# Mixer projections u, b and the two gates as feature-major seven-product units on 256 tokens each

## The chip, the cores and the metric

The kernel runs on one core of one Trainium2 chip. The metric is the device time of one execution in microseconds (us). A core has a matrix engine (TensorE; PE in the profile, with its weight loads counted apart as PEld), a vector engine (VectorE, DVE), a scalar engine (ScalarE, ACT), a general engine (GpSimd, POOL) and a queue engine for transfers (SyncE, SP), which run side by side and wait for each other through semaphores. Products land in PSUM, which this kernel divides into 8 tiles of 128 x 512 float32.

## The reference, cut to what matters

512 tokens of 1024 features go through two attention layers, a feed-forward block, a mixer and a second feed-forward block. The change is in the mixer alone:

```python
z = h @ w_in                      # h: 512 x 1024, w_in: 1024 x 7168
za, zb, zg = split(z)             # u, v | gate_b, gate_c, xb | g_a, g_b, each 1024 wide
u, v = split(gelu(za))
y_a = spatial_gating(u, v) @ w_proj_a
y_b = (gate_b * short_conv(gate_c * xb)) @ w_proj_b
merged = sigmoid(g_a) * y_a + sigmoid(g_b) * y_b
out = merged @ w_out
```

## The kernel before, in words

Every float32 factor is held as two parts, a rounded one (`hi`) and what is left (`lo`). `mm3` makes a product from three matmuls of the same shape: hi x hi, hi x lo, lo x hi. Weights come from HBM in pieces of 1 MB into a ring of 5 raw tiles (`raw`). ScalarE writes `hi`, VectorE writes `lo = raw - hi`, each in tiles of 128 x 1024 with 4 buffers for each kind.

Two ways of making a projection stand in the mixer:

- Direct and feature-major (`fm1`): a weight block of 128 x 128 is stationary and all 512 tokens of the activations move past it. One output tile of 128 features is 8 x 3 matmuls of 512 columns in one PSUM tile. In before, u (`u_job`), gate_b (`b_job`) and both gates (`gated_job`) are made so. `gated_job` loads the gate's block and the block of `w_proj_a` or `w_proj_b` in one piece.
- In seven products instead of eight (`block_jobs`): the activations and weights are cut two by two, sums of blocks are formed, and seven products give the four result blocks. In before, v and gate_c with xb (`v_unit`, `cx_unit`) are made so, token-major, with 512 columns moving. The sums of activation blocks (`bt`, `bn`, and one that is put over part of `xg` by `t4_parts`) are there already. Since u, b and the gates need `xg` as it was, `block_b12` writes that part back at the end of the second `cx_unit`.

`run` walks through a list of jobs. Before it issues a job's products it asks for the next job's weights. Small pieces of other work (`light`: the spatial gate, convolutions, transposes) are put in between at due times. The order of the list in the mixer is v, cx 0, cx 1, u, first gate with `w_proj_a`, b, second gate with `w_proj_b`, output. A planner then fixes each engine's order of instructions ahead of time, by a simulated timeline. It may put an instruction that is ready by that timeline ahead of one that isn't, and the order is kept on the chip. Temporary tiles of 128 x 512 come from a pool of 50 slots.

Of the kernel before, what the change touches and what calls it, by code (L numbers as in the profile page):

```python
# [41 lines left out]

NCOL = _layout()
ORDER = ('gv0 gv2 dz0 gq gz0 gz2 dz2', 'gk gv0 dz2 gv2 gq dz0 gz0 gz2')
SLOTS = 50
LAG = 1
GAP = (2.6, 2.0)
AHEAD = 10.0
# [24 lines left out]
TURN = 10.0  # L73
TURN0 = 1.5
REST = 12.0


@with_exitstack
def block_kernel(ctx: ExitStack, tc: tile.TileContext, a, out):
# [64 lines left out]
    def weights(src, shapes):  # L144

        total = sum(k * n for k, n in shapes)
        raw = wraw.tile([P, 2112], F32, tag="raw", name=nm("raw"))
        nc.sync.dma_start(raw[:, 0:total], src)
        at, pieces = 0, []
        for k, n in shapes:  # L150
            src_p = raw[:, at:at + k * n]
            hi = wsp.tile([P, 1024], F32R, tag="hi", name=nm("hi"))[:, 0:k * n]
            lo = wsp.tile([P, 1024], F32R, tag="lo", name=nm("lo"))[:, 0:k * n]
            A.activation(hi, src_p, AF.Copy)  # L154
            V.tensor_tensor(lo, src_p, f(hi), op=ALU.subtract)  # L155
            pieces.append(tuple(v.rearrange("p (k n) -> p k n", n=n) for v in (hi, lo, src_p)))
            at += k * n
        return pieces

    FM = [(KT, P)] * 2  # L160
    TM = [(2, S)] * 2
# [192 lines left out]
        A.activation(hi, e, AF.Copy)  # L354
        V.tensor_tensor(lo, e, f(hi), op=ALU.subtract)

    def block(name, p, t):

        tiles, at = {
            "b11": (lambda: st["xg"][2 * p], 0), "b21": (lambda: st["xg"][2 * p + 1], 0),  # L360
            "b22": (lambda: st["xg"][2 * p + 1], H), "t4": (lambda: st["xg"][2 * p], H),
            "t3": (lambda: st["bt"][p], 0), "t2": (lambda: st["bt"][p], H),
            "t1": (lambda: st["bn"][p // 2], p % 2 * H),
        }[name]
        return tuple(v[:, at + t * P:at + t * P + P] for v in tiles())

    def block_b12(p, nxt):

        hi, lo = (v[:, H:] for v in st["xg"][2 * p])
        x, g = xs[2 * p][:, H:], nxt(2 * p)  # L370
        A.activation(hi, x, AF.Copy, scale=g)
        V.scalar_tensor_tensor(lo, x, g, f(hi), op0=ALU.mult, op1=ALU.subtract)

    def block_jobs(src, hook, turn=False):


        q, banks = {}, {}

        def load(name, i):
            q[name] = wraw.tile([P, 2112], F32, tag="raw", name=nm("raw"))[:, 0:4 * S]  # L380
            nc.sync.dma_start(q[name], src[i])

        def parts(name, turn=False):
            pieces = []
            for j in range(2):
                r = q[name][:, 2 * j * S:2 * j * S + 2 * S]
                hi, lo = (wsp.tile([P, 1024], F32R, tag=v, name=nm(v)) for v in ("hi", "lo"))
                A.activation(hi, r, AF.Copy)  # L388
                if turn:
                    A.activation(lo, r, AF.Copy, scale=-1.0)  # L390
                    nc.gpsimd.dma_start(lo, r, accum_op=ALU.add)
                else:
                    V.tensor_tensor(lo, r, f(hi), op=ALU.subtract)  # L393
                pieces.append(tuple(v.rearrange("p (k n) -> p k n", n=S) for v in (hi, lo)))
            return pieces

        def l1():
            load("a11", 0)
            load("a21", 2)
            nc.gpsimd.dma_start(q["a21"], q["a11"], accum_op=ALU.add)  # L400
            return parts("a11", turn)

        def l2():
            load("a22", 3)
            return parts("a21")

        def l3():
            load("a12", 1)
            return parts("a21")

        def sums(i):

            if i == 0:
                V.tensor_tensor(q["a21"], q["a21"], q["a22"], op=ALU.add)
            if i == 1:
                V.tensor_tensor(q["a11"], q["a21"], q["a11"], op=ALU.subtract)

        def l4():
            nc.gpsimd.dma_start(q["a21"], q["a12"], accum_op=ALU.add)
            return parts("a11")  # L420


        steps = [
            (l1, "b11", "a", True), (l2, "t3", "b", True), (l3, "t2", "a", False), (l4, "t1", "a", False),
            (lambda: parts("a12"), "b21", "c", True), (lambda: parts("a22"), "t4", "b", False),
            (lambda: parts("a21"), "b22", "a", False),
        ]

        def step(i, name, chain, first):
            def body(ps):  # L430
                if first:
                    banks[chain] = [psum("tm") for _ in range(2)]
                for t in range(2):
                    for p in range(4):
                        ah, al = block(name, p, t)
                        wh, wl = (v[:, p % 2] for v in ps[p // 2])
                        mm3(banks[chain][t], ah, al, wh, wl, first and p == 0, p == 3, True)
                        yield 0.68
                    hook(i, t, banks)
                    if t == 0:  # L440
                        sums(i)
            return body

        return [(ld, None, step(i, *which)) for i, (ld, *which) in enumerate(steps)]


    mods = [(const.tile([P, 24], F32, name=f"mod{l}"), const.tile([P, 8], F32, name=f"gs{l}")) for l in range(L)]
# [788 lines left out]
    def mixer_jobs():  # L1236
# [66 lines left out]
        def cx_unit(n):  # L1303
            v, h = {}, {}

            def hook(i, t, banks):
# [6 lines left out]
                if i == 5:  # L1313
                    V.scalar_tensor_tensor(v[0, t], v[2, t], roots("nrs2", t), v[0, t], op0=ALU.mult, op1=ALU.mult)
                    h[t] = v[0, t]
                    if t == 1 and n == 1:
                        for p in range(4):
                            block_b12(p, gains)
                if i == 6:
                    V.scalar_tensor_tensor(v[3, t], v[3, t], roots("nrs2", 2 + t), banks["a"][t], op0=ALU.mult, op1=ALU.mult)  # L1320
                    h[2 + t] = v[3, t]
# [1 line left out]
                        light(conv(n, h), TURN)  # L1323

            return block_jobs(a["mcx"][n], hook)

        jobs += v_unit()
        for n in range(2):
            jobs += cx_unit(n)

        def gate(h, u):
            b, hb = h // 4, slice((h % 4) * P, (h % 4 + 1) * P)
# [8 lines left out]
            ya[h] = split(u, "ya")  # L1341
            yield 0.9, 0

        def u_job(c):
            def body(ps):
                if c == 0:
                    spatial()
                for j in range(2):
                    h = 2 * c + j
                    o = psum("fm")  # L1350
                    yield from fm1(o, [ps[j]], st["xg"])
                    u = slot("mu")
                    V.tensor_tensor(u, o, st["bc"], op=ALU.mult)
                    A.activation(u, u, AF.Gelu_apprx_tanh)
                    light(gate(h, u), 9.0 if h < 2 else 2.0)
            return body

        jobs += [(a["mu"][c], FM, u_job(c)) for c in range(4)]


        def gated_job(which, i, acts):
            def body(ps):
                o = psum("fm")
                yield from fm1(o, [ps[0]], st["xg"])
                t = slot("mgt")
                V.tensor_tensor(t, o, st["bc"], op=ALU.mult)
                A.activation(t, t, AF.Tanh, scale=0.5)
                while len(acts) < KT:
                    yield None
                pr = psum("fm")  # L1370
                yield from fm1(pr, [ps[1]], acts)
                V.scalar_tensor_tensor(t, t, 1.0, pr, op0=ALU.add, op1=ALU.mult)
                if which == 0:
                    ma.append(t)
                else:
                    V.tensor_tensor(t, t, ma[i], op=ALU.add)
                    mer.append(split(t, "mm"))
            return body

        jobs += [(a["mgp"][0, i], FM, gated_job(0, i, ya)) for i in range(KT)]  # L1380

        def b_job(c):
            def body(ps):
                for j in range(2):
                    o = psum("fm")
                    yield from fm1(o, [ps[j]], st["xg"])
                    g = slot("mgb")
                    V.tensor_tensor(g, o, st["bc"], op=ALU.mult)
                    while len(cv) <= 2 * c + j:
                        yield None  # L1390
                    V.tensor_tensor(g, g, cv[2 * c + j], op=ALU.mult)
                    yb.append(split(g, "yb"))
            return body

        jobs += [(a["mb"][c], FM, b_job(c)) for c in range(4)]
        jobs += [(a["mgp"][1, i], FM, gated_job(1, i, yb)) for i in range(KT)]

        def o_job(c):
            def body(ps):
# [19 lines left out]
def _pack(i):  # L1419
# [65 lines left out]
    w = i["w_in_2"][0]  # L1485
    mu, mv, mb, mc, mx, ga, gb = (w[:, D * j:D * j + D] for j in range(7))
    r["mv"] = c(blocks(mv[:, 0:S], mv[:, S:]))
    r["mu"], r["mb"], r["mo"] = c(cols256(mu)), c(cols256(mb)), c(cols256(i["w_out_2"][0]))

    def pairs(p, q):  # L1490
        return np.stack([tiles(np.concatenate([p[:, P * j:P * j + P], q[:, P * j:P * j + P]], axis=1)) for j in range(8)])

    r["mcx"] = c(np.stack([blocks(mc[:, j:j + S], mx[:, j:j + S]) for j in (0, S)]))
    r["mgp"] = c(np.stack([pairs(ga, i["w_proj_a_2"][0]), pairs(gb, i["w_proj_b_2"][0])]))
    r["sgu_wT"] = c(i["sgu_w_2"][0].transpose(2, 0, 1).reshape(P, 2, 4 * P).transpose(1, 0, 2))
    r["sgu_b"] = c(i["sgu_b_2"][0])
    return r
# [18 lines left out]
```

## Time and profile before

| | |
|---|---|
| median of 3 runs | 1693.03 us (1692.37 to 1694.29) |
| the profiled execution | 1691.1 us |
| its span, first to last instruction | 1689.3 us |
| TensorE busy | 1647.6 us, 98% of the span, 8080 matmuls |
| VectorE busy | 1127.6 us, 67% |
| ScalarE busy | 807.7 us, 48% |
[...]

Busy time is the time in which the engine had at least one instruction in work, as the profiler's records say. The records of matmuls overlap (one lasts longer than the distance to the next), so the pace of matmuls is read from their starts or from their number in a stretch, not from the duration of one. In the trace the mixer lies from about 905 us (first v product) to about 1339 us.

### The profile page before, as it was taken

How to read it: one execution, taken by the hardware profiler on the slowest of the kernel's cores; microseconds unless marked ns; L12 is line 12 of the kernel's file. 1: busy time of each engine (PE TensorE's matmuls, PEld its weight loads, DVE VectorE, ACT ScalarE, POOL GpSimd, SP SyncE). 2: the span in 40 equal slices, each digit the busy share in tenths (PEclk: the TensorE clock that was granted, in tenths of full speed). 3: DMA queues.
4: the chain of work that ended last, by engine and by line, in shares of the span. 5: the costliest groups of instructions: out<-in, count | busy, mean ns of one | idle time of the engine just before them, and what ended most of it. 6: DMA issues, size and time to landing. Idle time of an engine off the chain costs nothing.

```text
span 1689.3 us, 20507 instructions
## 1 busy us (share of the span) xinstructions
PE 1647.6 (98%) x8080; PEld 1363.9 (81%) x8080; DVE 1127.6 (67%) x1648; ACT 807.7 (48%) x1343; POOL 113.6 (7%) x102
## 2 busy tenths in 40 slices
PE   6997999999999999999999999999999999999998
PEld 5785788897778888888888888888888888888887
DVE  8889866778765865755768887534545775765754
ACT  4564565446655543533556654322233553542543
POOL 3120010330000000000002100000000000000000
PEclk9998999999999999999999999999999999999999
DMA  8535412342213163553554653222222334561521
GB/s 313 202 131 194 163 63 76 126 150 75 75 51 94 50 181 115 159 165 97 151 161 109 165 173 126 79 96 100 100 100 100 93 109 122 149 199 51 162 88 50
DMA packets 32161, 209.73 MB, mean 124 GB/s; under 512 B 3617, under 2 KB 3777, under 8 KB 8641
## 3 DMA queue, kind: packets, MB, share of 16 engines
q1 hardware_dynamic: 28032, 180.11, 29.8%
q0 software_dynamic: 4032, 28.31, 8.7%
q8 instruction: 63, 1.03, 0.2%
q14 instruction: 34, 0.27, 0.0%
HBM read 178.00 MB, written 2.10 MB: 107 GB/s over the span
## 4 chain that ended last, share of the span: by engine, by line
PE 91%; DVE 4%; ACT 2%; DMA 1%; issue 0%; POOL 0%; SPq 0%; POOLq 0%; DVEq 0%; ACTq 0%
PE fm L179 16%; PE fm L181 16%; PE fm L180 16%; PE tm L179 12%; PE tm L181 12%; PE tm L180 12%; PE ht L1100 1%; PE sc L838 1%; DVE ada L482 1%; PE o L874 1%; DVE cv L598 1%; DVE lo L155 1%; DMA ada<-in_ada 1%; PE go L994 0%; PE ot L537 0%
## 5 line engine op out<-in xcount | busy, mean ns | idle before, releaser
L154 ACT ACTIVATE hi<-raw 128x1024 fp32r<-128x1024 f32 (+2 forms) x184 | 187.9, 1024 | 350.5 <-PE fm L180 277.1
L393 DVE TENSOR_TENSOR lo<-raw,hi 128x1024 fp32r<-128x1024 f32 x180 | 218.2, 1223 | 89.4 <-ACT hi L388 88.0
L388 ACT ACTIVATE hi<-raw 128x1024 fp32r<-128x1024 f32 x182 | 191.4, 1057 | 174.4 <-PE tm L181 89.7
L155 DVE TENSOR_TENSOR lo<-raw,hi 128x1024 fp32r<-128x1024 f32 (+2 forms) x184 | 216.6, 1179 | 44.2 <-ACT hi L154 37.5
L179 PE MATMUL tm<-hi,xgh 128*128 128x512 f32 x480 | 177.9, 393 | 12.4 <-ACT hi L639 12.4
L180 PE MATMUL tm<-lo,xgh 128*128 128x512 f32 x480 | 187.7, 393 | 0.2 <-DVE lo L640 0.2
L181 PE MATMUL tm<-hi,xgl 128*128 128x512 f32 x480 | 185.2, 392 | 0.0
L179 PE MATMUL fm<-fhh,hi 128*128 128x512 f32 (+1 forms) x368 | 140.0, 383 | 0.0
L180 PE MATMUL fm<-fhl,hi 128*128 128x512 f32 (+1 forms) x368 | 139.9, 380 | 0.0
L181 PE MATMUL fm<-fhh,lo 128*128 128x512 f32 (+1 forms) x368 | 139.9, 380 | 0.0
L179 PE MATMUL fm<-xgh,hi 128*128 128x512 f32 x320 | 125.9, 393 | 0.0
L180 PE MATMUL fm<-xgl,hi 128*128 128x512 f32 x320 | 124.4, 389 | 0.0
L181 PE MATMUL fm<-xgh,lo 128*128 128x512 f32 x320 | 124.4, 390 | 0.0
L179 PEld LDWEIGHTS tm<-hi,xgh 128*128 128x128 f32 x480 | 90.4, 189 | 31.7 <-ACT hi L639 12.9
L179 PE MATMUL fm<-hh,hi 128*128 128x512 f32 x256 | 108.8, 428 | 6.8 <-DVE gs L487 4.5
L180 PEld LDWEIGHTS tm<-lo,xgh 128*128 128x128 f32 x480 | 91.1, 190 | 19.7 <-DVE lo L640 0.7
L181 PEld LDWEIGHTS tm<-hi,xgl 128*128 128x128 f32 x480 | 90.9, 190 | 18.8
L181 PE MATMUL fm<-hh,lo 128*128 128x512 f32 x256 | 103.1, 403 | 0.0
L180 PE MATMUL fm<-hl,hi 128*128 128x512 f32 x256 | 102.9, 402 | 0.0
L181 PEld LDWEIGHTS fm<-fhh,lo 128*128 128x128 f32 x368 | 69.2, 188 | 13.2
L180 PE MATMUL tm<-lo,bth 128*128 128x512 f32 x208 | 79.9, 392 | 0.0
L180 PEld LDWEIGHTS fm<-fhl,hi 128*128 128x128 f32 x368 | 69.3, 188 | 12.7
(313 smaller groups left out, 3434.0 us busy)
## 6 DMA issues: line engine op xcount, KB each, us to landing
raw<-in_ffs SPq DMA_DIRECT2D x40, 1024.0 KB, 5.0
raw<-raw POOLq DMA_DIRECT2D x26, 1024.0 KB, 8.0
ada<-in_ada SPq DMA_DIRECT2D x23, 1024.0 KB, 4.8
raw<-in_wfm SPq DMA_DIRECT2D x16, 1024.0 KB, 4.8
raw<-in_ffo SPq DMA_DIRECT2D x16, 1024.0 KB, 4.9
raw<-in_mgp SPq DMA_DIRECT2D x16, 1024.0 KB, 4.8
raw<-in_wo SPq DMA_DIRECT2D x8, 1024.0 KB, 4.8
raw<-in_mcx SPq DMA_DIRECT2D x8, 1024.0 KB, 5.8
```

The costliest lines, as they stand in the source:

```text
L154: A.activation(hi, src_p, AF.Copy)
L155: V.tensor_tensor(lo, src_p, f(hi), op=ALU.subtract)
L179: T.matmul(o, wh, ah, start=start, stop=False, skip_group_check=open)
L180: T.matmul(o, wh, al, start=False, stop=False, skip_group_check=open)
L181: T.matmul(o, wl, ah, start=False, stop=stop, skip_group_check=open)
L388: A.activation(hi, r, AF.Copy)
L393: V.tensor_tensor(lo, r, f(hi), op=ALU.subtract)
L482: V.scalar_tensor_tensor(w[:, i], w[:, i], 1.0, cact, op0=ALU.mult, op1=ALU.mult, accum_out=t[:, j + i:j + i + 1])
L598: V.scalar_tensor_tensor(c[:, sh:S], ps[:, 0:S - sh], tap[3 - sh], c[:, sh:S], op0=ALU.mult, op1=ALU.add)
L838: T.matmul(pss[m][:, 0:n], qk[hd][0][p][r, i * P:(i + 1) * P], qk[hd][1][q_][r, 0:n], start=p + q_ == 0, stop=False)
L874: T.matmul(on[hd][:, i * P:(i + 1) * P], et[:, j * P:(j + 1) * P], vt[j][:, hd * P:(hd + 1) * P], start=j == 0, stop=j == i)
L1100: T.transpose(ps[:, t * P:(t + 1) * P], h[t][:, c * P:(c + 1) * P], ident)
```

## The change

u, b and the two gates (16 pieces of 256 output features) become feature-major units of seven products, `fm_unit`. A unit holds a weight piece in four quarters: input features in even and odd blocks of 128, and two blocks of 128 output features. Each product is 4 input blocks x 3 matmuls, with a weight block of 128 x 128 stationary and 256 tokens moving (`block` gets a width). The sums of weight quarters are made by two accumulating transfers of GpSimd's queue, 256 KB each, and two subtractions and additions of VectorE. Three PSUM tiles x, y, z take the seven products in the order x, y, x, z, x, y, x, and in between x, y and z are read out and combined into two result tiles of 512 tokens.

The projections `w_proj_a` and `w_proj_b` become pieces and jobs of their own (`plain`, `p_job`), still made directly with 512 columns. The order becomes v, then u and first gate mixed (`UG`), `w_proj_a`, cx 0, cx 1, b, second gate, `w_proj_b`, output. Each item's transfer is issued inside the item before it (`linked`). `block_b12` goes. The pool grows from 50 to 56 slots, and the scratch area for GpSimd's transfer descriptors is set to 4096 bytes to make room. The amounts loaded from HBM stay the same.

The core of the diff:

```diff
-SLOTS = 50
+SLOTS = 56
+UG = ('u0', 'u1', 'g0', 'u2', 'g1', 'u3', 'g2', 'g3')
...
-        return tuple(v[:, at + t * P:at + t * P + P] for v in tiles())
-
-    def block_b12(p, nxt):
-
-        hi, lo = (v[:, H:] for v in st["xg"][2 * p])
-        x, g = xs[2 * p][:, H:], nxt(2 * p)
-        A.activation(hi, x, AF.Copy, scale=g)
-        V.scalar_tensor_tensor(lo, x, g, f(hi), op0=ALU.mult, op1=ALU.subtract)
+        return tuple(v[:, at + t * P:at + t * P + n] for v in tiles())
...
+    def fm_unit(src, begin, finish):
+        q, v = {}, {}
+
+        def parts(at, n):
+            r = q["r"][:, at:at + n]
+            hi, lo = (wsp.tile([P, 1024], F32R, tag=t, name=nm(t))[:, 0:n] for t in ("hi", "lo"))
+            A.activation(hi, r, AF.Copy)
+            V.tensor_tensor(lo, r, f(hi), op=ALU.subtract)
+            return tuple(w.rearrange("p (k n) -> p k n", n=P) for w in (hi, lo))
+
+        def quarter(i):
+            return q["r"][:, i * S:(i + 1) * S]
+
+        def load():
+            q["r"] = wraw.tile([P, 2112], F32, tag="raw", name=nm("raw"))[:, 0:4 * S]
+            nc.sync.dma_start(q["r"], src)
+            nc.gpsimd.dma_start(quarter(1), quarter(0), accum_op=ALU.add)
+
+        def first():
+            a = parts(0, 2 * S)
+            V.tensor_tensor(quarter(1), quarter(1), quarter(3), op=ALU.add)
+            V.tensor_tensor(quarter(0), quarter(1), quarter(0), op=ALU.subtract)
+            q["s"] = parts(0, 2 * S)
+            return a, q["s"]
+
+        def second():
+            a = parts(2 * S, 2 * S)
+            nc.gpsimd.dma_start(quarter(1), quarter(2), accum_op=ALU.add)
+            return a, parts(S, S)
+
+        def product(o, w, at, name, start):
+            for p in range(4):
+                ah, al = block(name, p, 0, H)
+                mm3(o, w[0][:, at + p], w[1][:, at + p], ah, al, start and p == 0, p == 3, True)
+                if p % 2:
+                    yield 0.72
+
+        def one(ps):
+            begin()
+            for k in "xyz":
+                v[k] = psum("fu")[:, 0:H]
+            v[0], v[1] = slot("fa"), slot("fb")
+            yield from product(v["x"], ps[0], 0, "b11", True)
+            A.activation(v[0][:, 0:H], v["x"], AF.Copy)
+            yield from product(v["y"], ps[0], 4, "t3", True)
+            yield from product(v["x"], ps[1], 4, "t2", False)
+            A.activation(v[1][:, 0:H], v["x"], AF.Copy, scale=-1.0)
+
+        def two(ps):
+            yield from product(v["z"], ps[0], 0, "b21", True)
+            V.tensor_tensor(v[0][:, 0:H], v[0][:, 0:H], v["z"], op=ALU.add)
+            yield from product(v["x"], q["s"], 0, "t1", False)
+            A.activation(v[1][:, H:], v["x"], AF.Copy, scale=-1.0)
+            V.tensor_tensor(v[1][:, H:], v[1][:, H:], v["y"], op=ALU.subtract)
+            yield from product(v["y"], ps[0], 4, "t4", False)
+            V.tensor_tensor(v[1][:, 0:H], v[1][:, 0:H], v["y"], op=ALU.subtract)
+            yield from product(v["x"], ps[1], 0, "b22", False)
+            yield from finish(v[0], v["x"], v[1])
+
+        return load, [(first, None, one), (second, None, two)]
...
+    def rooted(u, last, v):
+        V.tensor_tensor(u[:, 0:H], u[:, 0:H], st["bc"][:, 0:H], op=ALU.mult)
+        V.tensor_tensor(u[:, H:], last, st["bc"][:, H:], op=ALU.mult)
+        V.tensor_tensor(v, v, st["bc"], op=ALU.mult)
...
-                    if t == 1 and n == 1:
-                        for p in range(4):
-                            block_b12(p, gains)
...
+        def u_unit(c):
+            def finish(u, last, v):
+                rooted(u, last, v)
+                for j, t in enumerate((u, v)):
+                    A.activation(t, t, AF.Gelu_apprx_tanh)
+                    light(gate(2 * c + j, t), 9.0 if c == 0 else 2.0)
+                yield 0
+            return fm_unit(a["mu"][c], spatial if c == 0 else lambda: None, finish)
...
+        def g_unit(which, c):
+            def finish(u, last, v):
+                if which == 1 and c > 1:
+                    for k in range(0, 2) if c == 2 else range(2, KT):
+                        yb.append(split(cv[k], "yb"))
...
+                rooted(u, last, v)
+                for t in (u, v):
+                    A.activation(t, t, AF.Tanh, scale=0.5)
+                    gates[which].append(t)
...
+        def b_unit(c):
+            def finish(u, last, v):
+                rooted(u, last, v)
...
+                for k, t in ((2 * c, u), (2 * c + 1, v)):
+                    V.tensor_tensor(cv[k], cv[k], t, op=ALU.mult)
...
+        items = [(None, v_unit())]
+        for which in UG:
+            items.append((u_unit if which[0] == "u" else lambda c: g_unit(0, c))(int(which[1])))
+        items += [plain(a["mp"][0, c], p_job(0, c, ya)) for c in range(4)]
+        items += [(None, cx_unit(n)) for n in range(2)]
+        items += [b_unit(c) for c in range(4)] + [g_unit(1, c) for c in range(4)]
+        items += [plain(a["mp"][1, c], p_job(1, c, yb)) for c in range(4)]
+        jobs += linked(items)
...
-    nc = bacc.Bacc("TRN2", target_bir_lowering=False, num_devices=1)
+    nc = bacc.Bacc("TRN2", target_bir_lowering=False, num_devices=1, dynamic_dma_scratch_size=4096)
```

## Rows read from the trace of the kernel before

**Rows 1.** The page, part 1: busy us (share of the span), instructions.

```profile
span 1689.3 us, 20507 instructions
PE 1647.6 (98%) x8080; PEld 1363.9 (81%) x8080; DVE 1127.6 (67%) x1648; ACT 807.7 (48%) x1343; POOL 113.6 (7%) x102
```

**Rows 2.** Stretches of the mixer: length, busy us (instructions) of PE, PEld, DVE, ACT, POOL, clock.

```profile
943.00:981.00 38.00, 38.00 (x169) 31.45 (x168) 28.21 (x31) 23.14 (x29) 3.66 (x5) 1.00 0.59 167
981.00:1018.00 37.00, 37.00 (x173) 30.54 (x172) 31.39 (x36) 19.84 (x26) 0.86 (x1) 1.00 0.55 171
1077.00:1164.00 87.00, 87.00 (x385) 72.03 (x384) 31.25 (x33) 21.64 (x25) 0.00 (x0) 1.00 0.26 92
```

**Rows 3.** Waits of PE from 525 to 1665 us: the only row.

```profile
PE tm L179 <- ACT bth L169: 1.0, 1, 1.0
```

**Rows 4.** Groups of matmuls by shape: busy us, mean ns of one.

```profile
L179 PE MATMUL fm<-xgh,hi 128*128 128x512 f32 x320 | 125.9, 393 | 0.0
L180 PE MATMUL fm<-fhl,hi 128*128 128x256 f32 x32 | 9.1, 285 | 0.0
```

**Rows 5.** The stretch of the last job's 54 matmuls of 256 columns.

```profile
1665.41:1671.88 6.47, 6.47 (x55) 6.46 (x54) 2.66 (x5) 2.12 (x5) 0.00 (x0) 1.00 0.01 3
```

**Rows 6.** Timeline of PE in the first cx unit: start, us, instruction.

```profile
957.77 0.62 PE L179 MATMUL tm<-hi,xgh 128*128 128x512 f32 x2
958.22 0.39 PE L179 MATMUL tm<-hi,bnh 128*128 128x512 f32 x1
...
960.71 0.39 PE L181 MATMUL tm<-hi,bnl 128*128 128x512 f32 x1
960.94 0.39 PE L180 MATMUL tm<-lo,xgh 128*128 128x512 f32 x1
```

**Rows 7.** Groups of DVE instructions in the mixer, by shape.

```profile
L155 DVE TENSOR_TENSOR lo<-raw,hi 128x1024 fp32r<-128x1024 f32 x60 | 73.4, 1223 | 7.6 <-ACT hi L154 7.3
...
L1337 DVE SCALAR_TENSOR_TENSOR mw<-sg,cols,sgub 128x512 f32<-128x512 f32 x8 | 6.0, 749 | 6.4 <-PE sg L1335 6.3
...
L170 DVE TENSOR_TENSOR yal<-mu,yah 128x512 fp32r<-128x512 f32 x8 | 5.5, 690 | 4.2 <-ACT yah L169 4.2
...
L339 DVE TENSOR_TENSOR te<-te 128x256 f32<-128x256 f32 x5 | 2.1, 424 | 0.1
```

**Rows 8.** Groups of ACT instructions in the mixer, by shape.

```profile
L154 ACT ACTIVATE hi<-raw 128x1024 fp32r<-128x1024 f32 x60 | 63.7, 1061 | 177.5 <-PE fm L180 163.5 <-issue 7.8 <-PE fm L181 3.5
...
L169 ACT ACTIVATE yah<-mu 128x512 fp32r<-128x512 f32 x8 | 5.0, 628 | 18.5 <-DVE mu L1340 18.5
...
L346 ACT ACTIVATE bnh<-te 128x256 fp32r<-128x256 f32 x5 | 2.0, 403 | 0.8 <-DVE te L339 0.8
```

**Rows 9.** Timeline of DVE: two weight splits one behind the other.

```profile
967.74 2.35 DVE L393 TENSOR_TENSOR lo<-raw,hi 128x1024 fp32r<-128x1024 f32 x2
```

**Rows 10.** Timelines of ACT and of DVE: a read of PSUM and its user.

```profile
961.14 0.60 ACT L1309 ACTIVATE ca<-tm 128x512 f32<-128x512 f32 x1 [1.63 <-PE tm L181]
961.77 0.69 DVE L1312 TENSOR_TENSOR ca<-ca,tm 128x512 f32<-128x512 f32 x1 [1.00 <-ACT ca L1309]
```

**Rows 11.** Transfers by issue (KB each, median us to landing), and POOL's group of issues.

```profile
raw<-raw POOLq DMA_DIRECT2D x26, 1024.0 KB, 8.0
...
raw<-in_mgp SPq DMA_DIRECT2D x16, 1024.0 KB, 4.8
...
lo<-raw POOLq DMA_DIRECT2D x2, 512.0 KB, 4.5
...
L400 POOL DMA_DIRECT2D raw<-raw x13 | 11.3, 872 | 566.0 <-DVE lo L155 375.2 <-DMA raw<-in_ffs 104.8 <-DMA raw<-in_mv 31.6
```

**Rows 12.** Timelines: issue of the b weights on SP, first b matmul on PE.

```profile
1096.41 32.97 SPq L148 DMA_DIRECT2D raw<-in_mb  x4
...
1159.31 0.39 PE L179 MATMUL fm<-xgh,hi 128*128 128x512 f32 x1
```

**Rows 13.** The chain that ended last: one head's spatial gate.

```profile
1048.37 0.89 PE sg L1335 x8
```

More of the change, by code (lines that the diff above doesn't have):

```diff
@@ L148, in weights, with pieces @@
         nc.sync.dma_start(raw[:, 0:total], src)
-        at, pieces = 0, []
+        return pieces(raw, shapes)
+    def pieces(raw, shapes):
+        at, out = 0, []
         for k, n in shapes:
@@ L155, in weights @@
             V.tensor_tensor(lo, src_p, f(hi), op=ALU.subtract)
-            pieces.append(tuple(v.rearrange("p (k n) -> p k n", n=n) for v in (hi, lo, src_p)))
+            out.append(tuple(v.rearrange("p (k n) -> p k n", n=n) for v in (hi, lo, src_p)))
             at += k * n
-        return pieces
+        return out
     FM = [(KT, P)] * 2
@@ L355, in t4_parts, with block @@
         V.tensor_tensor(lo, e, f(hi), op=ALU.subtract)
-    def block(name, p, t):
+    def block(name, p, t, n=P):
         tiles, at = {
@@ new lines, in plain, with load, linked @@
+    def plain(src, body):
+        q = {}
+        def load():
+            q["r"] = wraw.tile([P, 2112], F32, tag="raw", name=nm("raw"))
+            nc.sync.dma_start(q["r"][:, 0:4 * S], src)
+        return load, [(lambda: pieces(q["r"], FM), None, body)]
+    def linked(items):
+        jobs = []
+        for i, (load, own) in enumerate(items):
+            if i == 0 and load is not None:
+                own[0] = (lambda load=load, f=own[0][0]: (load(), f())[1],) + own[0][1:]
+            if i + 1 < len(items) and items[i + 1][0] is not None:
+                k = max(0, len(own) - 2) if len(own) > 2 else len(own) - 1
+                own[k] = (lambda f=own[k][0], load=items[i + 1][0]: (f(), load())[0],) + own[k][1:]
+            jobs += own
+        return jobs
@@ L1325, in cx_unit @@
             return block_jobs(a["mcx"][n], hook)
-        jobs += v_unit()
-        for n in range(2):
-            jobs += cx_unit(n)
         def gate(h, u):
@@ L1342, in gate @@
             yield 0.9, 0
-        def u_job(c):
-            def body(ps):
[L1346 to L1367, printed above, removed]
+        def u_unit(c):
[6 more added lines that the diff above has]
+            return fm_unit(a["mu"][c], spatial if c == 0 else lambda: None, finish)
@@ new lines, in mixer_jobs @@
+        gates = [[], []]
+        def g_unit(which, c):
[3 more added lines that the diff above has]
+                        yb.append(split(cv[k], "yb"))
+                    if c == 3:
+                        cv.clear()
+                rooted(u, last, v)
+                for t in (u, v):
+                    A.activation(t, t, AF.Tanh, scale=0.5)
+                    gates[which].append(t)
+                yield 0
+            return fm_unit(a["mg"][which, c], lambda: None, finish)
@@ L1368, in body, with p_job @@
+        def p_job(which, c, acts):
+            def body(ps):
                 while len(acts) < KT:
                     yield None
[L1370 to L1377, printed above, removed]
-            return body
@@ L1380, in mixer_jobs @@
[L1380 to L1393, printed above, removed]
@@ L1395, in mixer_jobs @@
-        jobs += [(a["mb"][c], FM, b_job(c)) for c in range(4)]
-        jobs += [(a["mgp"][1, i], FM, gated_job(1, i, yb)) for i in range(KT)]
+                for j in range(2):
+                    t = gates[which].pop(0)
+                    pr = psum("fm")
+                    yield from fm1(pr, [ps[j]], acts)
+                    V.scalar_tensor_tensor(t, t, 1.0, pr, op0=ALU.add, op1=ALU.mult)
+                    if which == 0:
+                        ma.append(t)
+                    else:
+                        V.tensor_tensor(t, t, ma.pop(0), op=ALU.add)
+                        mer.append(split(t, "mm"))
@@ new lines, in p_job @@
+            return body
+        def b_unit(c):
+            def finish(u, last, v):
+                rooted(u, last, v)
+                while len(cv) <= 2 * c + 1:
+                    yield None
+                for k, t in ((2 * c, u), (2 * c + 1, v)):
+                    V.tensor_tensor(cv[k], cv[k], t, op=ALU.mult)
+            return fm_unit(a["mb"][c], lambda: None, finish)
+        items = [(None, v_unit())]
+        for which in UG:
+            items.append((u_unit if which[0] == "u" else lambda c: g_unit(0, c))(int(which[1])))
@@ L1487, in _pack, with blocks256 @@
     r["mv"] = c(blocks(mv[:, 0:S], mv[:, S:]))
-    r["mu"], r["mb"], r["mo"] = c(cols256(mu)), c(cols256(mb)), c(cols256(i["w_out_2"][0]))
-    def pairs(p, q):
-        return np.stack([tiles(np.concatenate([p[:, P * j:P * j + P], q[:, P * j:P * j + P]], axis=1)) for j in range(8)])
+    def blocks256(w):
+        t = lambda j, e: w[:, j:j + P].reshape(KT, P, P)[e::2].transpose(1, 0, 2).reshape(P, -1)
+        return np.stack([np.concatenate([t(j + P * i, e) for e in range(2) for i in range(2)], axis=1) for j in range(0, D, 2 * P)])
+    r["mu"], r["mb"], r["mo"] = c(blocks256(mu)), c(blocks256(mb)), c(cols256(i["w_out_2"][0]))
     r["mcx"] = c(np.stack([blocks(mc[:, j:j + S], mx[:, j:j + S]) for j in (0, S)]))
-    r["mgp"] = c(np.stack([pairs(ga, i["w_proj_a_2"][0]), pairs(gb, i["w_proj_b_2"][0])]))
+    r["mg"] = c(np.stack([blocks256(ga), blocks256(gb)]))
+    r["mp"] = c(np.stack([cols256(i["w_proj_a_2"][0]), cols256(i["w_proj_b_2"][0])]))
     r["sgu_wT"] = c(i["sgu_w_2"][0].transpose(2, 0, 1).reshape(P, 2, 4 * P).transpose(1, 0, 2))
```

## The prediction

> **What bounds the kernel now.** I read the page first. TensorE is busy for 98% of the span, VectorE for 67% [rows 1], so the question is whether the changed stretch is TensorE's to the end. The stretches of the mixer say yes: in the cx unit, in the second cx unit and in the first gate with its projection PE is busy for every microsecond, though DVE is busy for 28.21 of 38 and even 31.39 of 37 us [rows 2]. The waits of PE confirm it: from 525 to 1665 us they come to 1.0 us, one wait at the head of the v unit [rows 3]. So a matmul saved in the mixer is time saved, as long as its replacements' weights and evacuations keep up; DVE and the transfers cost nothing until they make PE wait. [...]
>
> **The pace of a matmul.** The record of one lasts longer than the distance to the next, so I count. The gate stretch holds 384 weight loads in 87.00 us [rows 2]: 0.2266 us for 512 columns (its record says 0.393 [rows 4]). The changed units need 256 columns, which occur in the last job: 54 weight loads in 6.47 us [rows 5], 0.1198 us (its record: 0.285 [rows 4]). Half the columns cost 53% of the time.
>
> **What goes and comes on PE.** u, b and both gates are 16 pairs of output tiles. Before: 2 x 8 x 3 = 48 matmuls of 512 columns a pair, 48 x 0.2266 = 10.88 us. After: 7 products x 4 blocks x 3 = 84 matmuls of 256 columns, 84 x 0.1198 = 10.06 us. Saved: 0.81 us a unit, 13.0 us in all. One product in eight is left out, but the shorter matmuls give back almost half of it. The projections with `w_proj`, v, cx, the spatial gates and the transposes keep their matmuls and only move.
>
> [...]
>
> [...]
>
> **What comes on DVE.** A unit's weights need three splits of 1024 (1.223 us), one of 512 (0.690), and two sums of 512 (I take the 0.690 row). The results need five operations on 256 columns (0.424, from SBUF, the nearest row) and one on 512 [rows 7]: 3 x 1.223 + 4 x 0.690 + 5 x 0.424 = 8.55 us, where a pair had 2 x 1.223 + 2 x 0.690 = 3.83. For u two gates come on top, 2 x (0.749 + 2 x 0.690) = 4.26 us.
> - u and first gate mixed: DVE 8 x 8.55 + 4 x 4.26 = 85.4 us, PE 8 x 10.06 + 8 gates x 0.89 [rows 13] = 87.6 us.
> - b and second gate: DVE 68.4 us, 16 products and `lo` splits with the convolution (11.0), and 8 taps of the second cx unit (0.749 each: 6.0), 85.4 us; PE 80.5 us. Here DVE is over by 4.9 us by its records.
>
> Records of DVE overlap too: two splits behind one another took 2.35 us, the second starting 1.13 after the first [rows 9], 7% less than 1.223. At that pace DVE needs 79.4 us and PE is the bound. Bounds of this loss: 0 and 4.9 us; I take 1.5, since a DVE that is never idle runs at the pace, but operations that depend on each other don't. On ACT a unit has 3.5 splits (1.061), three reads of 256 (0.403) [rows 8] and two functions, under 7 of 10 us: no bound.
>
> **The wait that the order adds.** In `two`, product t4 adds to y. It must not start before DVE has subtracted y, which waits for ACT's copy of x, which waits for t1, the product just before. Left as written PE would stand still for: the last matmul's tail, 0.285 - 0.120 = 0.16 [rows 4, 5]; ACT's read, 0.403 [rows 8]; DVE, 0.424 [rows 7]; and three handovers of some 0.03 to 0.05 (ACT's read ends at 961.74, DVE starts at 961.77 [rows 10]): 1.1 us a unit, more than the 0.81 saved. Queued behind t4 on PE is b22 and then the next unit. But the planner may fill. The first cx unit had a like case: the product with `bnh` had to wait for the read of its bank, and PE's order has matmuls of the later product (`xgh`) ahead of it and in between [rows 6], with no wait in the stretch [rows 2]. Here the next unit's b11 is there to fill: its buffers come free after t3, over 4 us earlier, and three units of x, y, z don't fit, but two do (6 of 8 PSUM tiles). So I put the stall at 0; its bounds are 0 and 1.1 us a unit, and if a 1.061 split and a 1.13 one always sat in front in the queues, 3.3. If the cover were gone, this alone would make the kernel slower.
>
> Other reads have a whole product of cover (12 x 0.120 = 1.44 us): x after b11 under t3, x after t2 under b21. ACT's 0.40 fits, even with one split of 1.06 before it (1.46).
>
> **Transfers.** HBM loads are the same 16 + 8 pieces, and run far ahead: the b weights were issued on SP at 1096.41, their first matmul came at 1159.31 [rows 12]. The chain SP 4.8, issue on POOL 0.87, and 256 KB (from 8.0 and 4.5 us for 1024 and 512 KB, a straight line gives an estimate of 2.8) [rows 11] is 8.5 us against that lead: hidden. The second accumulation sits between the sums' splits and the split for b22: 0.87 + 2.8 + ACT 0.63 [rows 8] + DVE 0.69 = 5.0 us, and b22 comes 8.6 us after the unit's start while its sums are split about then: 3.6 us to spare. POOL has 32 issues more, 28 us, in a stretch where it did next to nothing [rows 2]. Without cover each unit would wait up to the 5.0 us.
>
> **Slots and small parts.** 56 slots against roughly 53 to 55 live at the start of g2 and in the last gate unit; a wait for a slot would last at most one gate's chain, 0.89 + 0.75 + 0.69 + 0.63 + 0.69 = 3.7 us, once or twice. Value 0. `block_b12`, 4 x (0.40 + 0.42) by the rows of 256 columns, lay beside PE work: 0. The six `yb` splits in the last gate unit (6 x 0.69 = 4.1) must be done by the end of the first `w_proj_b` tile, 5.4 us later: 0.
>
> **Sum.** -13.0 + 1.5 = -11.5 us. The profiled execution took 1691.1 us (span 1689.3 and 1.8 around it), 1.9 under the median of the runs. 1691.1 - 11.5 = 1679.6, on the median 1693.0 - 11.5 = 1681.5 us.
>
> **Rivals and chances.** The runs of before lie within 0.1%; 0.2% (3.4 us) is about what a measurement of this kernel can tell from no change.
> - A, as summed, stalls of 0 to 4.9 us: -13.0 to -8.1, 1680.0 to 1684.9. For it: rows 2, 3 and 6. Chance 0.62.
> - B, some of the waits before t4 stay open, say half: 8 x 1.1 = 8.8 us, -4.2 us, 1688.8. The planner's times aren't the chip's, and DVE at 90% leaves little room. Chance 0.14.
> - C, slower: the wait before t4 is open in every unit. 16 x 1.1 = 17.6 us, +4.6, 1697.6; it turns at 0.81 us a unit. With both splits ahead in the queues, 16 x 3.3 - 13.0 = +39.8. Against it: PE's order in rows 6. Chance 0.10.
> - D, no change within 0.2%: C's stall at 0.6 to 1.0 us a unit. Chance 0.08.
> - E, faster than the sum: the 256-column pace is not the floor. The 128-column gate matmuls run at 0.89/8 = 0.111 us [rows 13]; 84 x 0.111 = 9.35, -24.5 us, 1668.5. Against it: 54 in a row at 0.1198. Chance 0.05. [...]
> - F, weight loads exposed: at the load engine's share, 6.46 of 6.47 us busy [rows 5], a load can't be later than its matmul. If the loads ran end to end at the 72.03/384 = 0.188 us of their records [rows 2], 84 x 0.188 = 15.8 us, +78 us. Rows 5 exclude it nearly: 0.01. [...]
>
> Faster 0.62 + 0.14 + 0.05 = 0.81, same 0.08, slower 0.11. Range: from 1679, one us of spread under A, to 1692, through B and into D, about 0.8; A's own is 1680 to 1685.
>
> **What would show it.** The matmuls of the units: 1344 of 256 columns, a stretch of units at 0.120 us each. PE's waits in the mixer: under 5 us; a row of waits for DVE's subtraction of y, 16 times, is C. DVE's share in the b and second gate stretch about 90%. The mixer's length 434 before, 422 after. Wrong would make it: a pace over 0.1295 us (10.88/84), which takes the whole gain, waits of DVE's `lo`, or of transfers on POOL.

## The result: slower, and the profile after

The changed kernel takes 1713.48 us (median of 4 runs, 1709.51 to 1714.8), before on the same chip 1693.11. The ratio is 1.0114, 95% interval 1.0101 to 1.0127: slower by 20 us, where 11.5 us less were forecast. The profiled execution took 1714.66 us.

The page, part 1, of the changed kernel, beside [rows 1]:

```profile
PE 1647.9 (96%) x8656; PEld 1388.4 (81%) x8656; DVE 1190.7 (70%) x1772; ACT 845.1 (49%) x1419; POOL 140.3 (8%) x134
```

576 matmuls more, as planned, but PE is busy for 96% where it was 98%: it stands still somewhere. The waits of PE from 525 to 1690 us, where before has one of 1.0 us [rows 3] (columns: total us, times, longest):

```profile
PE fu L183 <- ACT hi L451: 8.9, 14, 1.0
PE fu L183 <- ACT fb L493: 7.6, 3, 2.5
PE fu L185 <- DVE lo L452: 2.1, 4, 0.8
PE fu L183 <- ACT fa L490: 1.5, 1, 1.5
PE fm L183 <- ACT hi L158: 1.2, 1, 1.2
PE tm L183 <- ACT bth L173: 1.0, 1, 1.0
PE fm L185 <- DVE lo L159: 0.5, 1, 0.5
```

22.8 us, and two groups lead: weight splits (`hi`, L451) that come up to 1.0 us late in many places, and the read of x after t2 (L493), three times 2.5 us late. The subtraction of y ahead of t4 (L500), on which the slower rival rested, is not among them.

Where it lies is told by windows of the changed kernel: u with the first gate, b with the second gate, and the whole mixer (columns as in [rows 2]):

```profile
933.00:1048.00 115.00, 100.99 (x741) 96.53 (x740) 85.34 (x141) 59.22 (x93) 14.47 (x17) 0.96 0.46 124
1168.00:1266.00 98.00, 90.80 (x698) 86.52 (x696) 77.92 (x119) 44.80 (x70) 11.23 (x13) 1.00 0.45 122
908.90:1362.40 453.50, 430.41 (x2537) 381.35 (x2536) 323.15 (x459) 212.62 (x303) 40.79 (x42) 0.99 0.46 131
```

The mixer takes 453.5 us. In before it is 433.0 (from the first norm product ahead of it, at 905.3, to the first behind it, at 1338.4); 420.0 would be left after the 13.0 us of the matmuls, so 33.5 us were lost. They lie in the units: from the start of each of their 1344 matmuls to the start of the next one on PE it is 194.7 us in all, by my count of the trace, where 0.12 us each would be 161.3. And the first stretch has a granted clock of 0.96, where the windows of before [rows 2] have 1.00. The timeline of PE at the second of the three 2.5 us waits shows both (start, us, instruction, idle before it and its releaser):

```profile
1010.48 0.28 PE L184 MATMUL fu<-btl,hi 128*128 128x256 f32 x1
1010.60 0.28 PE L185 MATMUL fu<-bth,lo 128*128 128x256 f32 x1
1013.40 0.58 PE L183 MATMUL fu<-bnh,hi 128*128 128x256 f32 x1 [2.52 <-ACT fb L493]
1013.77 0.42 PE L184 MATMUL fu<-bnl,hi 128*128 128x256 f32 x1
1013.99 0.42 PE L185 MATMUL fu<-bnh,lo 128*128 128x256 f32 x1
...
1016.70 0.28 PE L183 MATMUL fu<-bth,hi 128*128 128x256 f32 x1
```

Before the wait the matmuls start 0.12 us apart, the pace that [rows 5] gave. After it they start 0.21 to 0.22 apart (0.37 after the first), with longer records: the granted clock from 1013.40 to 1016.50 is 0.50, where it was 1.00 before the wait (1010.00 to 1010.90). The 15 matmuls from 1013.40 to 1016.70 took 3.30 us in place of 1.80, so the wait cost 1.5 us more than itself. The same follows the other two: 0.50 from 985.90 to 989.20 and from 1040.91 to 1043.80.

Why the read was late is told by the chain that ended last, read from the last line, that wait's end, upwards (start, us, what):

```profile
1001.17 4.14 DMA raw<-raw
...
1005.87 1.05 ACT hi L451
1006.94 1.22 DVE lo L452
1008.17 0.33 DVE fa L497
1008.50 0.60 DVE yal L174
1009.10 0.66 DVE mw L1420
1009.76 0.60 DVE raw L466
1010.36 0.34 DVE fa L532
1010.70 0.61 DVE fb L1423
1011.33 0.63 ACT yah L173
...
1012.01 1.06 ACT hi L451
1013.07 0.28 ACT fb L493
1013.40 0.58 PE fu L183
```

PE had finished t2, and the read (L493) needed nothing else. But in ScalarE's order it stands behind a weight split (1.06) and the split of a gate (`yah`, 0.63), and that gate's product (L1423) is the seventh of a row of VectorE operations without a gap: a weight split, results of the unit, both spatial gates of the u unit, sums of weight quarters. The weight split is that of the sums and needs one of them from this row (L467, done at 1011.90), so both of the instructions ahead of the read waited for VectorE. By this chain the row began late because an accumulating transfer landed late. Two suspects, then: VectorE's burst where both gates meet the weights' work, and the transfers.

The transfer by itself, in a unit of the second stretch, by the timelines of PE, DVE, POOL and ACT. PE starts the unit, the sums of its quarters are split, the second accumulation is issued:

```profile
1220.92 0.39 PE L183 MATMUL fu<-xgh,hi 128*128 128x256 f32 x1 [0.93 <-ACT hi L451]
1225.69 1.23 DVE L452 TENSOR_TENSOR lo<-raw,hi 128x1024 fp32r<-128x1024 f32 x1 [0.94 <-ACT hi L451]
1227.21 0.87 POOL L473 DMA_DIRECT2D raw<-raw  x1 [10.45 <-DVE lo L452]
```

It lands, and ScalarE and VectorE go on:

```profile
1230.53 1.58 ACT L451 ACTIVATE hi<-raw 128x512 fp32r<-128x512 f32 x2 [1.51 <-DMA raw<-raw]
1231.20 0.69 DVE L452 TENSOR_TENSOR lo<-raw,hi 128x512 fp32r<-128x512 f32 x1 [0.85 <-ACT hi L451]
1232.02 0.37 ACT L499 ACTIVATE fb<-fu 128x256 f32<-128x256 f32 x1
1232.16 0.39 PE L183 MATMUL fu<-xgh,hi 128*128 128x256 f32 x1 [0.84 <-ACT hi L451]
```

POOL could not issue sooner than 1226.92: it waited for the split that reads the quarter before it is overwritten (L452). ScalarE stands idle for 1.51 us until the transfer lands. Its row holds two splits, one behind the other: that of the landed quarter (128x512) and, by the kernel's order, the first one of the next unit's weights (128x1024). PE's wait of 0.84 us ends with the second. It is not the head of b22, which writes x, since x is still being read then (L499, 1232.02 to 1232.39). So the late transfer reaches PE through ScalarE's order, by a split that needs nothing of it.

The prices of VectorE's operations came out as forecast, and a transfer took 3.3 us where I had 2.8 (groups of DVE in the changed mixer, beside [rows 7], and the transfers by issue, beside [rows 11]):

```profile
L452 DVE TENSOR_TENSOR lo<-raw,hi 128x1024 fp32r<-128x1024 f32 x48 | 58.4, 1222 | 20.0 <-ACT hi L451 19.8
L467 DVE TENSOR_TENSOR raw<-raw 128x512 f32<-128x512 f32 x16 | 10.9, 684 | 0.1
```

```profile
raw<-raw POOLq DMA_DIRECT2D x32, 256.0 KB, 3.3
```

### The profile page after: what moved, and what is told of

Same layout as the page of the kernel before. It is cut to its first block, busy times and chain, and to the rows that moved or that the text cites. A ratio compares the mean times of both kernels' runs of the same rounds, so it can differ in the third digit from the quotient of the medians.

```text
span 1712.9 us, 21933 instructions
## 1 busy us (share of the span) xinstructions
PE 1647.9 (96%) x8656; PEld 1388.4 (81%) x8656; DVE 1190.7 (70%) x1772; ACT 845.1 (49%) x1419; POOL 140.3 (8%) x134
## 4 chain that ended last, share of the span: by engine, by line
PE 83%; DVE 6%; DMA 4%; ACT 4%; issue 2%; POOL 1%; SPq 0%; POOLq 0%; DVEq 0%; ACTq 0%
PE fm L183 12%; PE fm L185 12%; PE fm L184 12%; PE tm L183 12%; PE tm L185 12%; PE tm L184 12%; PE fu L183 2%; DMA raw<-raw 1%; PE fu L184 1%; DMA ada<-in_ada 1%; PE fu L185 1%; DVE ada L572 1%; PE ht L1190 1%; ACT hi L451 1%; DMA raw<-in_mg 1%
## 5 line engine op out<-in xcount | busy, mean ns | idle before, releaser
L385 ACT ACTIVATE hi<-raw 128x1024 fp32r<-128x1024 f32 x182 | 191.7, 1058 | 193.5 <-PE tm L185 89.7
L390 DVE TENSOR_TENSOR lo<-raw,hi 128x1024 fp32r<-128x1024 f32 x180 | 218.3, 1223 | 91.3 <-ACT hi L385 89.7
L158 ACT ACTIVATE hi<-raw 128x1024 fp32r<-128x1024 f32 (+2 forms) x152 | 153.9, 1016 | 230.0 <-PE fm L184 162.9
L159 DVE TENSOR_TENSOR lo<-raw,hi 128x1024 fp32r<-128x1024 f32 (+2 forms) x152 | 177.4, 1169 | 43.1 <-ACT hi L158 36.6
L452 DVE TENSOR_TENSOR lo<-raw,hi 128x1024 fp32r<-128x1024 f32 x64 | 69.4, 1089 | 33.4 <-ACT hi L451 32.9
L183 PE MATMUL fu<-xgh,hi 128*128 128x256 f32 x256 | 73.3, 289 | 8.9 <-ACT hi L451 8.7
L451 ACT ACTIVATE hi<-raw 128x1024 fp32r<-128x1024 f32 x64 | 58.5, 947 | 46.8 <-DMA raw<-raw 16.9
L183 PE MATMUL tm<-hi,bth 128*128 128x512 f32 x208 | 78.9, 393 | 1.0 <-ACT bth L173 1.0
```

The source lines that it names most:

```text
L183: T.matmul(o, wh, ah, start=start, stop=False, skip_group_check=open)
```

## The experiments

Kernels on one chip share their runs of before (1692.7 to 1693.1 us). Line L473 is the second sum of weight quarters (by an accumulating transfer in the changed kernel), the line with `quarter(0)` the first.

**Which transfer costs.** Either sum or both go from the transfer to VectorE:

```diff
 # e1 and e3, in load() and first()
-            nc.gpsimd.dma_start(quarter(1), quarter(0), accum_op=ALU.add)
+            V.tensor_tensor(quarter(1), quarter(1), quarter(0), op=ALU.add)
 # e1 and e2, in second()
-            nc.gpsimd.dma_start(quarter(1), quarter(2), accum_op=ALU.add)
+            V.tensor_tensor(quarter(1), quarter(1), quarter(2), op=ALU.add)
```

Both (e1):

> Both sums of a unit that were accumulating transfers on GpSimd's queue are made by VectorE (two more tensor_tensor of 512 columns, 0.69 us each, 16 units). Theory T (the transfers land later than the fixed order of ScalarE and VectorE assumes, the splits that wait for them hold up the PSUM reads queued behind): PE's waits in the mixer fall from 22.8 to under 6 us, the three stretches at half clock go, and the time comes to 1680 to 1688 us. Rival D (VectorE has too much work in the unit stretches): 22 us more of VectorE work there make it no faster than 1713, rather 1715 to 1730 us. Rival O (x is read under the cover of one product only): PE still waits some 10 us for ScalarE's reads, 1695 to 1710 us.

Only the second (e2):

> Only the second sum of a unit (quarter 1 plus quarter 2) goes from an accumulating transfer to VectorE. T: this is the transfer in the middle of a unit; the three waits of 2.5 us for ScalarE's read of x with their stretches at half clock go (some 13 us), the late first splits of the second gate stay: 1695 to 1702 us. D: 11 us more of VectorE work, 1713 to 1722 us. O: no change, 1710 to 1715 us.

Only the first (e3):

> Only the first sum of a unit (quarter 1 plus quarter 0) goes from an accumulating transfer to VectorE; the second stays a transfer. T: the second one no longer stands behind a first one on GpSimd's queue that waits for its HBM load; some of the late splits go, the half-clock stretches stay: 1703 to 1711 us. D: 1713 to 1722 us. O: 1710 to 1715 us.

Measured: e1 1709.85 us (ratio 1.0102, 1.0086 to 1.0117), e2 1705.15 (1.007, 1.0052 to 1.0088), e3 1713.92 (1.0124, 1.0107 to 1.014). The second transfer costs some 8 us more than the VectorE work put in its place; with the first the exchange changes nothing. e1 is 4.7 us slower than e2, and why isn't shown: PE's listed waits come to some 17 us in both. None of T's times came (1680 to 1688, 1695 to 1702, 1703 to 1711), so late transfers are not the whole cause. The waits of PE in e2:

```profile
PE fu L183 <- ACT fb L493: 8.8, 4, 3.6
PE fu L183 <- ACT hi L451: 1.9, 3, 0.8
```

The row of `hi` falls from 8.9 us to 1.9, so most of that row is the transfer's. The late reads of x stay: they need no late transfer.

**The slots and the descriptor area** (e4), in the kernel before:

```diff
-SLOTS = 50
+SLOTS = 56
-    nc = bacc.Bacc("TRN2", target_bir_lowering=False, num_devices=1)
+    nc = bacc.Bacc("TRN2", target_bir_lowering=False, num_devices=1, dynamic_dma_scratch_size=4096)
```

> The kernel before, with nothing but the pool of 56 slots and the descriptor area of 4096 bytes. T, D and O all put the loss into the mixer's units: 1693 us, no change within 2 us. If the start of the kernel (3.4 us later at the mixer's head in the profile of the changed kernel) comes from the slots or the descriptor area, it is 1696 to 1697 us.

Measured 1693.73 us, ratio 1.0005 (0.9996 to 1.0015): by themselves, in the kernel before, they cost nothing.

**Is it ScalarE's order alone?** In e6 (on e2) VectorE writes the gate's rounded part, so that ScalarE has nothing of a gate ahead of the read:

```diff
-            ya[h] = split(u, "ya")
+            hi, lo = slot("yah", F32R), slot("yal", F32R)
+            V.tensor_copy(hi, u)
+            V.tensor_tensor(lo, u, f(hi), op=ALU.subtract)
+            ya[h] = hi, lo
```

> On top of e2 (second sum by VectorE, 1705.2 us): the hi part of a gated u tile is written by VectorE, so no split of a gate stands in ScalarE's queue any more; VectorE has 8 x 0.6 to 0.7 us more. Theory H (PE's three waits of about 3 us for ScalarE's read of x come from ScalarE's order: the read stands behind the gate's split, which waits for VectorE): those waits and the stretches at half clock go, 1690 to 1697 us. Rival D (a burst of VectorE work in the u units holds up everything): 5 us more work in the same bursts, 1705 to 1712 us. Rival O (a read of x under one product of 1.44 us is too tight by itself): 1703 to 1707 us.

Measured 1703.8 us (1.0068, 1.0053 to 1.0083), against e2's 1.0052 to 1.0088: nothing that the intervals tell apart. The wait stays:

```profile
PE fu L183 <- ACT fb L493: 7.4, 4, 2.5
```

That the gate's split in ScalarE's queue is the whole cause (H) has fallen. With it out of the way a weight split still stands between PE and the read, and that split waits for the same row of VectorE, as the chain of e6 shows ahead of its longest wait:

```profile
1032.18 0.61 DVE raw L467
...
1032.89 1.06 ACT hi L451
...
1034.28 0.47 PE fu L183
```

No run put the read itself ahead of the splits in ScalarE's order, which would be the direct test of that order.

**VectorE's burst.** In e7 (on e2) the second gate of each u unit is due 6 us after the first:

```diff
-                    light(gate(2 * c + j, t), 9.0 if c == 0 else 2.0)
+                    light(gate(2 * c + j, t), (9.0 if c == 0 else 2.0) + 6.0 * j)
```

> On top of e2: the second gate of each u unit is due 6 us later than the first, so that two gates don't meet in one burst. H and D both: the waits shrink, 1693 to 1701 us; O: 1703 to 1707 us.

In e8 (on e2) the units change places, gates as they were:

```diff
-UG = ('u0', 'u1', 'g0', 'u2', 'g1', 'u3', 'g2', 'g3')
+UG = ('u0', 'g0', 'u1', 'g1', 'u2', 'u3', 'g2', 'g3')
```

> On top of e2: the units in the order u0 g0 u1 g1 u2 u3 g2 g3 in place of u0 u1 g0 u2 g1 u3 g2 g3. D: fewer neighbouring u units, fewer bursts, 1695 to 1702 us. H: a gate unit follows a u unit as before and its reads stand behind the gates' splits, so no change, 1702 to 1708 us. O: 1703 to 1707 us.

In e9 (on e2) the spatial gate's scale, bias and product are left out, and one column is scaled in their place:

```diff
-            g = slot("mw")
-            V.scalar_tensor_tensor(
...
-            V.tensor_tensor(u, u, g, op=ALU.mult)
+            V.tensor_scalar(u[:, 0:1], u[:, 0:1], ps[:, 0:1], None, op0=ALU.mult)
```

> On top of e2: the arithmetic of the spatial gate on VectorE is left out (scale, bias and product with u; one column of u is scaled so that the matmuls of the gate still have a reader), 8 x 1.4 us less on VectorE and no wait of the gate's split for it. H and D: the three long waits and the half-clock stretches go, 1688 to 1695 us. O: they stay, 1702 to 1706 us.

Measured: e7 1696.18 us (1.002, 1.0011 to 1.003), e8 1705.7 (1.0081, 1.0066 to 1.0096), e9 1694.59 (1.0016, 1.0007 to 1.0025). e7 and e9 came as H and D had them and not as O; e8 did not come as D had it. A date takes 9.0 us off e2, nearly as much as leaving the gates' two operations out (10.6); this other order of the units does nothing. The waits for L493 in e7:

```profile
PE fu L183 <- ACT fb L493: 1.0, 2, 0.6
```

And windows of 935 to 1045 us, first of e2, then of e7:

```profile
935.00:1045.00 110.00, 97.47 (x730) 94.03 (x729) 85.16 (x142) 56.92 (x89) 7.44 (x9) 0.95 0.31 99
```

```profile
935.00:1045.00 110.00, 103.69 (x795) 99.28 (x795) 91.33 (x153) 59.26 (x94) 7.85 (x10) 1.00 0.38 121
```

In e7 VectorE is busy for 91.33 of these 110 us and PE waits less than in e2, where VectorE has 85.16. So VectorE's total was no bound; what cost was when its work came. The clock is back at 1.00. What is shown is that the dates take these waits away; since the planner fixes the whole order anew, other instructions moved with them, and a part of the 9.0 us may be theirs.

**Do the two causes add up, and does more distance give more?** e10 is the changed kernel with e7's dates and the transfer kept. e11 is e7 with `9.0 + 12.0 * j` for every unit. e12 is e7 with the second sum as an addition by GpSimd:

```diff
-            V.tensor_tensor(quarter(1), quarter(1), quarter(2), op=ALU.add)
+            nc.gpsimd.tensor_tensor(quarter(1), quarter(1), quarter(2), op=ALU.add)
```

> The changed kernel, with the second gate of each u unit due 6 us after the first; both sums of weight quarters stay accumulating transfers. If the burst of VectorE work and the second transfer are two losses that add up, the gates apart give about 9 us here too (1705.15 - 1696.18 with the second sum on VectorE): 1713.5 - 9 = 1704.5 us, and the waits for the read of x after t2 (2.5 us each) go, with the half clock behind them, while the waits for hi behind a transfer stay. If the transfer is what makes the reads late, the gates' dates do nothing here and the time stays at 1713.

> The second sum by VectorE, and the gates of every u unit due 9 and 21 us after the unit, in place of 2 and 8 (first unit 9 and 15). If what is left in the stretch of u and first gate (8.5 us over the pace of the matmuls) still comes from gates that meet the weight splits, the wider distance takes up to 5 us of it: 1691 to 1694. If it comes from the splits of the next unit's weights alone (one and the same in units without a gate), nothing changes: 1696. If later gates only move the burst, it is slower, up to 1700.

> Gates apart, and the second sum of each unit by a GpSimd addition, neither by VectorE nor by a transfer: VectorE has 16 x 0.69 = 11 us less to do. If VectorE's load is what is left, up to 5 us faster than 1696.2, so 1691 to 1694. If what costs is a second piece of work on GpSimd's queue behind the first accumulation of a later unit, it goes back to the changed kernel's loss: 1696 + 8 = 1704 us, with waits for hi behind raw. If GpSimd's addition itself is slow (no row shows it), 1704 or more, with the record of it over 3.3 us.

Measured: e10 1707.75 us (1.0086, 1.0073 to 1.0099), e11 1693.32 (0.9999, 0.9991 to 1.0008), e12 1698.05 (1.0028, 1.0017 to 1.0039). In e10 the waits are:

```profile
PE fu L183 <- ACT hi L451: 8.8, 14, 1.0
PE fu L183 <- ACT fb L493: 2.5, 1, 2.5
```

The dates give 5.7 us with the transfer and 9.0 without it. Each of the two changes helps with and without the other, by intervals that don't meet: two causes. Whether their prices overlap isn't shown, since 3.2 us of difference are less than the spread of the runs of the changed kernel (5.3) and of e2 (4.5). By the mixers of the profiled executions, one each, they give 4.3 and 11.1. e10 lies between its two forecasts, 1704.5 and 1713. With the transfer one read is still late, and the row of `hi` is that of the changed kernel. e11 takes 2.9 us off e7, as forecast. e12 is no gain and lies between its forecasts; GpSimd's addition is slower than VectorE's 0.684 us (group of POOL):

```profile
L473 POOL TENSOR_TENSOR raw<-raw 128x512 f32<-128x512 f32 x16 | 27.0, 1687 | 92.6 <-DVE lo L452 92.6
```

**The best version** (e13), e11 with a gate's unit behind v:

```diff
-UG = ('u0', 'u1', 'g0', 'u2', 'g1', 'u3', 'g2', 'g3')
+UG = ('g0', 'u0', 'u1', 'g1', 'u2', 'u3', 'g2', 'g3')
```

> The kernel with the second sum by VectorE and the gates due 9 and 21 us after their unit, with the order of units g0 u0 u1 g1 u2 u3 g2 g3 in place of u0 u1 g0 u2 g1 u3 g2 g3: a gate's unit, without spatial gates, stands behind v. In the kernel before this one PE waits 1.5 us in the first unit for ScalarE's read of x, behind six scalings of v (3.78 us in one go). If the place behind v makes that wait, these scalings run into any first unit and nothing changes: 1693.3 us. If it is the first u unit's own call for v's scalings, they come a unit later, where nothing of v's is left to do, and 1.5 to 2.5 us go: 1691 to 1692. If three u gates now fall together with the last units, it is slower, up to 1697.

Measured 1691.76 us, ratio 0.9992 (0.9983 to 1.0001): not told apart from before, nor from e11. The reason that I gave for a gain has fallen, since the wait behind v's scalings stays:

```profile
PE fu L185 <- DVE lo L452: 2.1, 3, 1.2
PE fu L183 <- ACT fa L490: 1.5, 1, 1.5
PE fu L183 <- ACT hi L451: 1.1, 2, 0.7
```

## Why the prediction was wrong

**The pace and the matmuls: right.** 1344 matmuls of 256 columns, 0.12 us apart when nothing disturbs them. In e13 I counted the distances from each one's start to the next: 1295 of the 1344 are at 0.12 (within 0.05). So 13.0 us of matmuls were saved. Rival F, weight loads end to end at 0.188 us, didn't come: each of these matmuls has a load of its own, 0.191 to 0.197 us by the means of their records in the changed kernel, and starts 0.12 us after the one before it.

**VectorE's work: right in size, wrong in kind.** With 1.222, 0.684 and 0.416 us for its operations the 8.55 us a unit hold. The term of 1.5 us with bounds 0 and 4.9, worked out from the sum over a stretch, asked the wrong question: e7 has more VectorE work a microsecond (91.33 us in the 110 above, e2 85.16) and less waiting. What I had said of operations that depend on each other shows in before: the gate's product (L1340, 1036.89) starts 0.79 us after the operation whose output it takes (L1337, 1036.10, record 0.75), while the two splits of [rows 9] start 1.13 apart with a record of 1.223. The mixer of 422 us that I named as the mark of a right forecast came out at 453.5, and PE's waits, marked at under 5 us, at 22.8.

**The wait before t4, my slower rival: it didn't come.** No wait for L500 stands in the list. The sign of the result was that of the rival, its mechanism wasn't.

**"Other reads have a whole product of cover": the step that failed first.** I allowed the read of x one split of 1.06 ahead of it in ScalarE's queue, 1.46 us. That sum was over the cover of 1.44 already, and left out the last matmul's tail of 0.16. In the run the queue ahead of the read held two instructions, and both waited for a burst of VectorE. Measured, 3 waits, 7.6 us. In the same argument I left the clock out: three times 1.5 us, 4.5 in all. Dates for the gates give 5.7 us back with the transfer (e10, where one of the waits stays) and 9.0 without it (e7).

**"Transfers: hidden", "3.6 us to spare": the second step that failed.** The 256 KB took 3.3 us where I had 2.8, but that is not it: my chain began at the unit's start. In the unit shown above VectorE released the quarter at 1226.92, 6.0 us after the unit's first matmul. With the chain of 5.0 us behind it the split for b22 was done at 1231.89, 11.0 us after the start, where I had b22 at 8.6: 2.4 us late in place of 3.6 to spare. And ScalarE, idle for the transfer, holds up the splits and reads behind it. Taking it out is worth 8.3 us without the dates (e2) and 11.6 with them (1707.75 - 1696.18). Exchanging the first transfer for VectorE work gains nothing (e3), which agrees with its being hidden, as I had it.

**Slots, descriptor area: 0, as forecast** (e4, in the kernel before).

**The sum.** 1713.48 - 1696.18 = 17.3 of the 20.4 us come from these two causes, wider dates bring 2.9 more. Then the kernel equals before, and the gain of 13.0 us is still not there. By profiled mixers: before 433.0, e11 from 903.8 to 1336.0, 432.2, e13 from 909.0 to 1340.7, 431.7 us. Of the missing 11.7 us in e13 the list of PE's waits names 5.7 (its whole sum, 6.7, less the old 1.0). Of the loss in e13, 9.5 us lie in the units (170.8 us for their 1344 steps, where 0.12 each would be 161.3). Besides the listed waits, 34 steps are 0.05 to 0.15 us too long, 3.4 us together, and 9 some 0.16, 1.4 us. Most of these are waits too, or the step behind one. A matmul's record lasts 0.28 us where the next one starts after 0.12, so a wait of some 0.15 us leaves no idle time in PE's records; the weight loads show it (waits of PEld in e13, 905 to 1345 us):

```profile
PEld fu L185 <- DVE lo L452: 3.6, 8, 1.5
PEld fu L183 <- ACT fb L499: 2.2, 8, 0.8
PEld fu L183 <- ACT hi L451: 1.9, 4, 0.9
```

That is 20 waits where PE's list has 6 for the same three. Of the 43 steps, 13 end with such a release, 2.0 us, and 19, 2.0 us, are the step just behind a wait, some 0.22 us long; for 11, 0.9 us, I found none. The largest group waits for the read of x after t1 (L499), which I had priced as a part of the wait before t4 and put at 0: in 8 units only four matmuls, 0.48 us, stand between t1 and the matmul that waits for it. No run tried to take these waits away, and some 2 us of the missing 11.7 lie outside the units' steps, unexplained. The profiled execution of after also begins its mixer 3.4 us later than that of before (908.7 against 905.3); since that start lies between 903.8 and 909.0 in the kernels here, whose work ahead of it is the same, I put it down to the execution.

## What to carry to other kernels

A unit that saves 0.8 us of matmuls puts several readers, splits and sums into each 10 us of other engines; count for every read of PSUM what stands ahead of it in its engine's fixed order and what that waits for, one step further back than the instruction in front. A free engine's total says little: here the same VectorE work cost 9 us more or less by the date of one small job. A transfer that sits between two operations of a unit (released by one split, awaited by the next) cost 8 to 12 us here, though exchanging one of the same size at the head of the unit gained nothing. And look for short waits in the weight loads too: in e13 PEld's list has 20 waits where PE's, whose matmuls have records of 0.28 us and start 0.12 us apart, has 6.

## What the hardware showed unasked

After the three waits of PE of 2.5 us in the changed kernel the granted clock went to 0.50 for 2.9 to 3.3 us, at once (1013.40, above) or after a few matmuls (the wait that ends at 985.19, slow from 985.90), so each cost 1.4 to 1.6 us more than itself, by the starts of the matmuls behind it. The length of one wait didn't settle it here. In e1 a wait of the same length, 2.52 us to 1013.91, is followed by a clock of 1.00, while behind three waits of 0.9 to 1.0 us the clock is 0.50 (windows of e1):

```profile
954.62:958.00 3.38, 3.38 (x19) 3.38 (x18) 1.39 (x2) 0.53 (x2) 0.00 (x0) 0.50 0.53 225
1013.91:1017.30 3.39, 3.38 (x28) 3.39 (x29) 2.32 (x3) 1.77 (x4) 0.00 (x0) 1.00 0.00 0
```

In e10 a clock of 0.50 lasted from 985.05 to 991.80, twice as long, after a wait of 2.52 us and through one of 0.96. In the changed kernel an accumulating transfer of 256 KB took 3.3 us to land, one of 1024 KB 8.5 us (medians of 32 and 26).
